# Delta-rule gates computed by channel and applied as the output leaves PSUM, with another fixed order of heads and dense blocks

## The chip, the core and the metric

The kernel runs on one core of a Trainium2 chip. A core has five engines with queues of their own: TensorE (matmuls and, beside them, weight loads), VectorE, ScalarE, GpSimd and SyncE, which issues the DMAs. Each engine works through its queue in program order. The metric is the device time of one execution in microseconds; the times given are medians of several runs, and the profile is of one further execution.

## What is computed

One decoder block for 512 tokens and a width of 1024: a Mamba-2 SSD mixer (8 groups) and a gated-delta-rule mixer (8 pairs of heads) side by side, merged by sigmoid gates, then a squared-ReLU MLP. The part that the change touches is the end of the delta-rule mixer, cut here to what matters:

```python
def gated_deltanet_branch(qkv, z, b, a, conv_w, dt_bias, A_log, norm_w):
    qkv = jax.nn.silu(causal_depthwise_conv(qkv, conv_w))
    ...
    o = gated_delta_rule_chunked(q, k, v, g, beta)      # (B, S, 16 heads, 128)
    o = rmsnorm(o, norm_w) * jax.nn.silu(z.reshape(Bsz, S, GDN_N_V_HEADS, GDN_HEAD_V).astype(f32))
    return o.reshape(Bsz, S, GDN_VAL_DIM).astype(z.dtype)
```

Here `z` is a slice of the input projection `h @ w_in`, and `norm_w` has one number for each of the 128 channels of a head. For each token and head the output is divided by its root mean square, multiplied by the channel's weight and by `silu(z)`.

## The kernel before

Weights and activations are float32. A dense product is made of three matmuls of rounded parts (`mm3`, L149 to L152): high times high, low times high, high times low. Each weight tile of 128x1024 is loaded by a DMA, its high part is made by ScalarE (L469, `whi`) and its low part by VectorE (L471, `wlo`). Weights use three buffers in rotation.

The kernel has two stages. The second (L1197 on: up-projections, output projection, MLP) is plain code. The first, in which the mixers run, is written as a set of Python generators, the "streams", which issue instructions and yield what they cost and what they wait for. A planner (class `Weave`) runs these streams against its own table of costs (`A`, `V`, `G`, `PE`, `DM`) while the kernel is built. At each step it takes the stream of the lowest rank that is ready in its own time. The order in which instructions are issued this way is fixed for every engine; on the chip nothing is reordered. Costs in the table thus move no work by themselves, but they decide which instruction stands ahead of which.

The streams, by rank: loads and normalisation at the front; `prologue` (decays); `heads(gdn_scan, ssd_scan)`, the scans one after the other; `heads(gdn_end, ssd_end)`, their ends; `heads(gdn_prep, ssd_prep)`, their preparation; `weights`, which loads and splits weights in the order in which they are used; `early_ch`, six dense blocks accumulated while inputs still arrive; last `dense`, the filler of TensorE.

There are 16 heads: 0 to 7 are pairs of delta-rule heads, 8 to 15 SSD groups. `ORDER` says in which order they go through scan, end and preparation. `SEQ` is the order of the dense blocks: `i3` is the input of the head at place 3 of `ORDER` (four blocks of 128 channels by 512 tokens, each followed by a convolution of four taps), `z3` its gate, and `g0` to `g12` are blocks of the merge gates, which only go to DRAM and can stand anywhere. Three more blocks of that kind (L1231 on) are done at the start of the second stage.

What ties dense blocks to heads: `dense_in` waits for the scan of the head four places ahead (L566), `dense_z` for the end of the head three places ahead (L597), since gates have three buffers. `gdn_end` and `ssd_end` wait for the gate of their own head.

A delta-rule head: `gdn_prep` transposes keys, queries and values and forms the matrices; `solve` inverts 32x32 blocks on GpSimd (L825, L827), between a DMA through DRAM (`btd`, then `Nb`, L816, one buffer) and another one back (`ubd`, then `U`, also one buffer, which waits for the scan before); `gdn_scan` (L858 to L947) extends the inverse to 128 rows and carries the state over four chunks; `gdn_out` adds up the outputs `o` (tokens on partitions). `gdn_end` then makes the norm `ro` (one number per token and head) and, in eight operations of VectorE (L999), multiplies `o` by `ro` and by the gate `zs`. TensorE transposes the product to channels (L1005), and `put_y` takes it out of PSUM on ScalarE with the channel's weight as its scale (L715) and sends it to DRAM (L718). An SSD head ends in the same way with operations of its own (L1156 to L1172, then `put_y`).

The gate block `dense_z` computes `zs` with tokens on partitions: for each of four groups of 128 tokens the activations are the stationary operand and 256 columns of the weight are moving, so a head takes 4 x 8 x 3 = 96 matmuls of 256 columns. `z_end` (L622) applies the SiLU. At the end of the last gate blocks the plan puts two sums of `w_ada` (L485, L487, on VectorE) between the weights of `z15` and the next dense weight.

Of the kernel before, what the change touches and what calls it, by code (L numbers as in the profile page):

```python
# [10 lines left out]
F32 = mybir.dt.float32  # L11
F32R = mybir.dt.float32r
AF = mybir.ActivationFunctionType
# [4 lines left out]
ADD, SUB, MUL, MAX, POW = ALU.add, ALU.subtract, ALU.mult, ALU.max, ALU.pow  # L18
# [3 lines left out]
P = 128  # L22
T = 512
NC = 4
D = 1024
KD = 8
EPS = 1e-6
NEG = -1e30
CC, CB, CN1, CN2, CSB, CAL, CSN, CGN, CCV = 0, 8, 40, 48, 56, 57, 58, 74, 75
NCOL = CCV + 64 * 5  # L30
ORDER = (0, 8, 1, 2, 9, 3, 10, 4, 11, 5, 12, 6, 7, 13, 14, 15)
SEQ = ("i0 g0 g1 g2 i1 z0 i2 z1 g3 g4 i3 z2 i4 z3 i5 z4 i6 z5 i7 z6 i8 z7 i9 z8 i10 z9 i11 z10 i12 z11 i13 z12 i14 z13 i15 z14 g5 g6 g7 z15 g8 g9 g10 g11 g12")


class Weave:
# [62 lines left out]
def A(n, k=1, f="A"):  # L98
    return f, k * (0.27 + n / 1330)


def V(n, k=1):
    return "V", k * (0.19 + n / 975)
# [6 lines left out]
def PE(t):  # L110
    return "P", t
# [5 lines left out]
def hybrid_block(ctx: ExitStack, tc: tile.TileContext, x, cols, drow, rows, w_ada, w_ch, w_z,  # L117
                 w_up, w_out, w_mu, w_md, out):
    nc = tc.nc
    sc, ve, gp, pe = nc.scalar, nc.vector, nc.gpsimd, nc.tensor  # L120
# [11 lines left out]
    col = const.tile([P, NCOL], F32, name="col")  # L132
# [16 lines left out]
    def mm3(ps, lhs, rhs, first, last):  # L149
        pe.matmul(ps, lhsT=lhs[0], rhs=rhs[0], start=first, stop=False)  # L150
        pe.matmul(ps, lhsT=lhs[1], rhs=rhs[0], start=False, stop=False)  # L151
        pe.matmul(ps, lhsT=lhs[0], rhs=rhs[1], start=False, stop=last)  # L152
# [49 lines left out]
    sp = mix.enter_context(tc.tile_pool(name="sp", bufs=2))  # L202
# [13 lines left out]
    hT = [(chan_tile(), chan_tile()) for _ in range(KD)]  # L216
    ssx = const.tile([P, NC], F32, name="ssx")
    rsx = const.tile([P, NC], F32, name="rsx")
    wv = Weave()
# [4 lines left out]
    def bank(tag):  # L224
        key = yield from wv.slot(tag, pb[tag])
        return key, (psd if tag == "ps" else pss).tile([P, T], F32, tag=tag, name=tag, bufs=pb[tag])
# [315 lines left out]
    pre, mid, gate = {}, {}, {}  # L542
# [52 lines left out]
    def dense_z(i):  # L595
        if at[i] > 2:
            yield [("end", before(i, 3))]  # L597
        zs = sp.tile([P, NC, 256], F32, tag="zs", name="zs", bufs=3)
        ws = []
        for h in range(2):  # L600
            yield [("z", i, h)]
            ws.append(wts.pop(("z", i, h)))
        for tp in range(2):
            bk, ps = yield from bank("ps")
            for th in range(2):
                ts = slice((2 * tp + th) * P, (2 * tp + th + 1) * P)
                for k in range(KD):
                    w = ws[k // 4]
                    ks = slice((k % 4) * 256, (k % 4 + 1) * 256)
                    mm3(ps[:, th * 256:(th + 1) * 256], (hT[k][0][:, ts], hT[k][1][:, ts]),  # L610
                        (w[0][:, ks], w[1][:, ks]), k == 0, k == KD - 1)
                    yield PE(0.36)
            wv.start(3, z_end(i, zs, tp, bk, ps))
        count()
        count()
# [3 lines left out]
            yield from {"in": dense_in, "z": dense_z, "g": dense_g}[kind](i)  # L619

    def z_end(i, zs, tp, bk, ps):
        sc.activation(zs[:, 2 * tp:2 * tp + 2, :], ps.rearrange("p (a b) -> p a b", a=2), AF.Silu)  # L622
        gate[i] = zs
        yield A(T, 1, "L")
        wv.mark(bk)
        wv.mark(("z", i, "end", tp))
# [82 lines left out]
        yield A(D, 1, "E")  # L709
        wv.mark(key)  # L710

    def put_y(slot, bk, ps, ncol):
        key = yield from wv.slot("y", 2)
        y = sp.tile([P, T], F32, tag="y", name="y", bufs=2)
        sc.activation(y, ps, AF.Copy, scale=ncol)  # L715
        yield A(T)
        wv.mark(bk)
        nc.sync.dma_start(out=ydr[slot], in_=y)  # L718
        yield DM
        wv.mark(key)  # L720
# [121 lines left out]
    def gdn_scan(hq):  # L842
# [11 lines left out]
        bk, ps = yield from bank("pb")  # L854
        Z1 = sp.tile([P, 8, 32], F32, tag="Z", name="Z1", bufs=1)
        for q in range(8):
            for b in (0, 64):
                pe.matmul(ps[b + 32:b + 64, q * 32:(q + 1) * 32], lhsT=btu[b:b + 32, q, b + 32:b + 64],  # L858
                          rhs=T6[b:b + 32, q, 0:32], start=True, stop=True, tile_position=(b, b + 32))
        yield PE(1.0)  # L860
        for b in (0, 64):
            sc.mul(Z1[b + 32:b + 64], ps[b + 32:b + 64, 0:256].rearrange("p (a b) -> p a b", a=8), -1.0)
        yield A(256, 2)
# [1 line left out]
        bk, ps = yield from bank("pb")  # L865
        for q in range(8):
            for b in (0, 64):
# [1 line left out]
                          rhs=U[b + 32:b + 64, q, b + 32:b + 64], start=True, stop=True, tile_position=(b + 32, b))  # L869
            pe.matmul(ps[32:64, 256 + q * 32:256 + (q + 1) * 32], lhsT=U[32:64, q, 32:64], rhs=Z1[32:64, q, :],  # L870
                      start=True, stop=True, tile_position=(32, 32))
        yield PE(1.55)
        ve.tensor_copy(out=T6[32:64, :, 0:32], in_=ps[32:64, 256:512].rearrange("p (a b) -> p a b", a=8))
        for b in (0, 64):
            ve.tensor_copy(out=U[b:b + 32, :, b + 32:b + 64], in_=ps[b:b + 32, 0:256].rearrange("p (a b) -> p a b", a=8))
# [2 lines left out]
        bk, ps = yield from bank("pb")  # L878
# [8 lines left out]
        bk, ps = yield from bank("pb")  # L887
# [9 lines left out]
        o = sp.tile([P, NC, 256], F32, tag="o", name="o")  # L897
        so = sp.tile([P, NC, 2], F32, tag="so", name="so", bufs=3)
        S = None
        for c in range(NC):  # L900
            if c:
                bk, psk = yield from bank("pb")
# [4 lines left out]
                for j in range(2):  # L907
                    js = slice(j * P, (j + 1) * P)
                    ve.scalar_tensor_tensor(out=r[:, js], in0=psk[:, js], scalar=neg[:, c, 2 * hq + j:2 * hq + j + 1],
                                            in1=vt[:, c, js], op0=MUL, op1=ADD)  # L910
                kqs = yield from wv.slot("qs", 2)
                qs = sp.tile([P, 256], F32, tag="qs", name="qs")
                for j in range(2):
                    js = slice(j * P, (j + 1) * P)
                    sc.activation(qs[:, js], psk[:, 256 + j * P:256 + (j + 1) * P], AF.Copy,
                                  scale=tok2[:, c, 32 + 2 * hq + j:33 + 2 * hq + j])
# [6 lines left out]
            for j in range(2):  # L923
                js = slice(j * P, (j + 1) * P)
# [9 lines left out]
            if c < NC - 1:  # L934
                yield V(256, 2)
                wv.mark(bku)
                bk, pst = yield from bank("pb")
# [3 lines left out]
                if c:  # L941
                    for j in range(2):
                        js = slice(j * P, (j + 1) * P)
                        hd = 32 + 2 * hq + j
                        ve.scalar_tensor_tensor(out=Sn[:, js], in0=S[:, js], scalar=elast[:, hd, c:c + 1],
                                                in1=pst[:, js], op0=MUL, op1=ADD)
# [31 lines left out]

    def gdn_end(hq):
        yield [("scan", hq)]  # L980
        for tp in range(2):
            yield [("z", hq, "end", tp)]
        for c in range(NC):
            yield [("o", hq, c, "end")]
        zs = gate.pop(hq)
        o, so, rq, ko = mid.pop(hq)
        rqb = rq[:, :, None].to_broadcast([P, NC, 2])
        ve.tensor_mul(out=so, in0=so, in1=rqb)
        ve.tensor_mul(out=so, in0=so, in1=rqb)
        ve.tensor_scalar(out=so, in0=so, scalar1=1.0 / P, scalar2=EPS, op0=MUL, op1=ADD)  # L990
        yield V(8, 3)
        ro = sp.tile([P, NC, 2], F32, tag="ro", name="ro")
        gp.tensor_tensor(out=ro, in0=so, in1=mhalf.rearrange("p (a b) -> p a b", a=NC), op=POW)
        yield ("G", 2.0)
        ve.tensor_mul(out=ro, in0=ro, in1=rqb)
        for c in range(NC):
            for j in range(2):
                js = slice(j * P, (j + 1) * P)
                ve.scalar_tensor_tensor(out=o[:, c, js], in0=o[:, c, js], scalar=ro[:, c, j:j + 1],  # L999
                                        in1=zs[:, c, js], op0=MUL, op1=MUL)  # L1000
            yield V(P, 2)
        for j in range(2):
            bk, ps = yield from bank("pb")
            for c in range(NC):
                pe.transpose(ps[:, c * P:(c + 1) * P], o[:, c, j * P:(j + 1) * P], ident)  # L1005
            yield PE(0.43)
            if j:
                wv.mark(ko)
            wv.start(3, put_y(2 * hq + j, bk, ps, col[:, CGN:CGN + 1]))
        wv.mark(("end", hq))  # L1010

    def ssd_prep(g):
        i = 8 + g
# [217 lines left out]
    for i in range(NG, 16):  # L1231
        ps = proj_ch(65 + i)
# [7 lines left out]
    for br in (1, 0):  # L1240
        if not br:
            ys = load_y(0)
        for m4 in range(2):
            pp = [lpsum() for _ in range(4)]
            for kq in range(4):
                for m2 in range(2):
                    w = dense_w(w_up[br, 2 * m4 + m2, kq])
                    for k in range(4):
                        kk = kq * 4 + k
                        for i in range(2):  # L1250
                            ws = slice(k * 256 + i * P, k * 256 + (i + 1) * P)
# [81 lines left out]
    for half in range(2):  # L1333
        tt = (2 * half, 2 * half + 1)
        for hf in range(2):
            for t in tt:
                pp[t, hf] = lpsum()
            for kp in range(4):
                w = dense_w(w_out[hf, kp])
# [21 lines left out]
    for q in range(4):  # L1361
        act = []
        for m in range(8):
            mm = q * 8 + m
            if mm < len(ups):
                ps = ups[mm][1]
# [158 lines left out]
```

## Time and profile before

| | |
|---|---|
| median of 3 runs | 1485.68 us (1484.53 to 1488.55) |
| the profiled execution | 1484.77 us |
| its span, first to last instruction | 1483.1 us |
| first stage up to the end of the early blocks | 0 to 69 us |
| rest of the first stage, to the last head's transposes | 69 to 878 us |
| second stage | 878 to 1483 us |
| mean granted TensorE clock | 0.996 of full speed |

Busy times are of one engine each and overlap. A group's row names the line, the engine, the operation, what is written and read and the shape, then the busy time, the mean duration of one, and the time that its engine stood idle before it with what ended that. A matmul's duration is longer than its distance to the next one, since matmuls are pipelined: the cost of one in a row of them is the distance between starts. A row of the waits gives who waited for whom, the total, how often and the longest.

### The profile page before, as it was taken

To read this page: it belongs to the slowest core of one execution; us is meant where nothing else is said; L and a number is where in the kernel's file an instruction comes from. 1 tells how busy PE (TensorE), PEld (TensorE's weight loads), DVE (VectorE), ACT (ScalarE), POOL (GpSimd) and SP (SyncE) were. 2 spreads that over 40 slices of the span, in tenths; PEclk is the share of its full clock that TensorE was granted. 3 is DMA by queue.
4 is the path that set the end of the run, shared out by engine and by line. 5 is a ranking of instruction groups with operands and counts; after the bars stand their busy time and mean duration, and the time that the engine had idled before them with its cause. 6 is when DMAs were issued, how large, how long until landed. Compare 5 with 4: busy or idle time off the path is not lost. (4 is left out here: it accounts for less than half of the span.)

```text
span 1483.1 us, 22692 instructions
## 1 busy us (share of the span) xinstructions
PE 1458.1 (98%) x8592; PEld 1241.0 (84%) x8592; DVE 862.5 (58%) x1522; ACT 732.6 (49%) x1379; POOL 370.2 (25%) x691
## 2 busy tenths in 40 slices
PE   9999999999999999999999899999999999999998
PEld 7788898879989889888888788888878888888886
DVE  3565577677767777676777634444477324343444
ACT  6575545673764747645665635333355333132232
POOL 3005444341814607336623410000011000000002
PEclk9999999999999999999999999999999999999999
DMA  9323434543434524344343449543372233223221
GB/s 360 127 97 118 150 103 125 128 137 97 151 119 138 158 81 151 121 116 138 116 137 119 158 170 331 175 156 127 110 239 88 97 100 100 89 96 99 93 95 69
DMA packets 87070, 199.47 MB, mean 134 GB/s; under 512 B 32504, under 2 KB 33024, under 8 KB 86960
## 3 DMA queue, kind: packets, MB, share of 16 engines
q1 hardware_dynamic: 86960, 198.01, 41.3%
q8 instruction: 68, 1.11, 0.3%
q14 instruction: 42, 0.34, 0.1%
HBM read 181.10 MB, written 16.88 MB: 133 GB/s over the span
## 5 line engine op out<-in xcount | busy, mean ns | idle before, releaser
L150 PE MATMUL ps<-hT,whi 128*128 128x512 f32 x688 | 285.7, 415 | 4.8 <-ACT whi L469 4.3
L151 PE MATMUL ps<-hT,wlo 128*128 128x512 f32 x688 | 269.8, 392 | 1.2 <-DVE wlo L471 1.2
L152 PE MATMUL ps<-hT,whi 128*128 128x512 f32 x688 | 269.9, 392 | 0.0
L146 DVE TENSOR_TENSOR wlo<-raw,whi 128x1024 fp32r<-128x1024 f32 x114 | 140.0, 1229 | 199.7 <-ACT whi L145 199.7
L145 ACT CAST whi<-raw 128x1024 fp32r<-128x1024 f32 x114 | 119.4, 1048 | 210.1 <-PE pl L151 61.9
L150 PE MATMUL ps<-whi,hT 128*128 128x256 f32 (+1 forms) x536 | 166.3, 310 | 2.2 <-ACT y L715 1.4
L471 DVE TENSOR_TENSOR wlo<-raw,whi 128x1024 fp32r<-128x1024 f32 x103 | 128.1, 1244 | 64.2 <-ACT whi L469 60.3
L150 PEld LDWEIGHTS ps<-hT,whi 128*128 128x128 f32 x688 | 129.9, 189 | 31.9 <-ACT whi L469 4.5
L152 PE MATMUL ps<-wlo,hT 128*128 128x256 f32 (+1 forms) x536 | 154.3, 288 | 0.6 <-DVE wlo L471 0.6
L151 PE MATMUL ps<-whi,hT 128*128 128x256 f32 (+1 forms) x536 | 153.8, 287 | 0.0
L152 PEld LDWEIGHTS ps<-hT,whi 128*128 128x128 f32 x688 | 129.7, 189 | 28.3
L151 PEld LDWEIGHTS ps<-hT,wlo 128*128 128x128 f32 x688 | 130.1, 189 | 25.8 <-DVE wlo L471 2.4
L469 ACT CAST whi<-raw 128x1024 fp32r<-128x1024 f32 x103 | 107.3, 1044 | 67.4 <-PE ps L152 47.1
L533 DVE SCALAR_TENSOR_TENSOR cv<-ps,col,cv 128x511 f32<-128x511 f32 (+1 forms) x180 | 133.0, 742 | 8.0 <-ACT cv L527 5.4
L150 PEld LDWEIGHTS ps<-whi,hT 128*128 128x128 f32 x536 | 102.1, 190 | 5.8 <-ACT y L715 1.6
L825 POOL TENSOR_TENSOR tm<-Ub,Nb 128x60 f32<-128x60 f32 (+24 forms) x248 | 93.7, 378 | 52.5 <-DMA Nb<-btd 37.6
L151 PEld LDWEIGHTS ps<-whi,hT 128*128 128x128 f32 x536 | 102.1, 190 | 2.2
L152 PEld LDWEIGHTS ps<-wlo,hT 128*128 128x128 f32 x536 | 101.8, 190 | 2.0 <-DVE wlo L471 0.8
L827 POOL TENSOR_TENSOR Ub<-Ub,tm 128x60 f32<-128x60 f32 (+24 forms) x248 | 95.0, 383 | 19.4
L1416 POOL TENSOR_TENSOR ya<-ya,gate 128x512 f32<-128x512 f32 x4 | 5.8, 1466 | 324.8 <-ACT junk L1414 324.8
L150 PE MATMUL pl<-hT,whi 128*128 128x512 f32 (+1 forms) x184 | 66.6, 363 | 1.0 <-DVE hT L195 1.0
L151 PE MATMUL pl<-hT,wlo 128*128 128x512 f32 (+1 forms) x184 | 66.1, 362 | 0.4 <-DVE wlo L146 0.4
(502 smaller groups left out, 3049.0 us busy)
## 6 DMA issues: line engine op xcount, KB each, us to landing
raw<-in_w_ch SPq DMA_DIRECT2D x81, 512.0 KB
raw<-in_w_ada SPq DMA_DIRECT2D x48, 512.0 KB
raw<-in_w_z SPq DMA_DIRECT2D x32, 512.0 KB
raw<-in_w_up SPq DMA_DIRECT2D x32, 512.0 KB
raw<-in_w_mu SPq DMA_DIRECT2D x32, 512.0 KB
raw<-in_w_md SPq DMA_DIRECT2D x32, 512.0 KB
dc<-acd SPq DMA_DIRECT2D x16, 512.0 KB
ydr<-y SPq DMA_DIRECT2D x32, 256.0 KB
```

The lines of the kernel that those rows point to most:

```text
L145: sc.copy(hi, raw)
L146: ve.tensor_sub(out=lo, in0=raw, in1=hi.bitcast(F32))
L150: pe.matmul(ps, lhsT=lhs[0], rhs=rhs[0], start=first, stop=False)
L151: pe.matmul(ps, lhsT=lhs[1], rhs=rhs[0], start=False, stop=False)
L152: pe.matmul(ps, lhsT=lhs[0], rhs=rhs[1], start=False, stop=last)
L469: sc.copy(hi, raw)
L471: ve.tensor_sub(out=lo, in0=raw, in1=hi.bitcast(F32))
L533: ve.scalar_tensor_tensor(out=t[:, s:], in0=ps[:, :T - s], scalar=col[:, o + k:o + k + 1], in1=t[:, s:], op0=MUL, op1=ADD)
L825: gp.tensor_tensor(out=t3, in0=Ub[:, 0:r, j:j + 1].to_broadcast([P, r, n]), in1=Nb[:, j:j + 1, j + 1:32].to_broadcast([P, r, n]), op=MUL)
L827: gp.tensor_tensor(out=Ub[:, 0:r, j + 1:32], in0=Ub[:, 0:r, j + 1:32], in1=t3, op=SUB)
L1416: gp.tensor_tensor(out=y, in0=y, in1=gates[1][:, hs], op=MUL)
```

## The change

Four things are changed.

- **Gates of delta-rule heads by channel.** For heads 0 to 7 `dense_z` makes the weight the stationary operand and moves 512 tokens, as the other dense blocks do. `zs` then has the channels on partitions, one 512-token row for each of the two heads of a pair. SSD heads keep their form.
- **The gate is applied on the way out of PSUM.** `gdn_end` multiplies `o` by the norm in two operations of 512 columns, ahead of its wait for the gate; `put_y` gets the gate as an argument and, for delta-rule heads, evacuates on VectorE: PSUM times the channel's weight times the gate. The mark that the head has ended is set there, once the second output has left PSUM, in place of the end of `gdn_end`.
- **Another fixed order.** `ORDER` puts delta-rule heads 0 to 4 first, then SSD heads 8 to 11, then 5, 6, 7, then 12 to 15. `SEQ` moves the gate blocks and spreads the g blocks: `z0` comes directly behind `g0`, and one g block, `g12`, follows `z15`, where five did.
- **Two costs in the planner's table** for the scan's first matmuls: 1.0 becomes 0.79, 1.55 becomes 0.65.

```diff
@@ -28,8 +28,9 @@
 NEG = -1e30
 CC, CB, CN1, CN2, CSB, CAL, CSN, CGN, CCV = 0, 8, 40, 48, 56, 57, 58, 74, 75
 NCOL = CCV + 64 * 5
-ORDER = (0, 8, 1, 2, 9, 3, 10, 4, 11, 5, 12, 6, 7, 13, 14, 15)
-SEQ = ("i0 g0 g1 g2 i1 z0 i2 z1 g3 g4 i3 z2 i4 z3 i5 z4 i6 z5 i7 z6 i8 z7 i9 z8 i10 z9 i11 z10 i12 z11 i13 z12 i14 z13 i15 z14 g5 g6 g7 z15 g8 g9 g10 g11 g12")
+ORDER = (0, 1, 2, 3, 4, 8, 9, 10, 11, 5, 6, 7, 12, 13, 14, 15)
+SEQ = ("i0 g0 z0 g1 g2 i1 i2 g3 z1 i3 g4 z2 g5 i4 i5 z3 g6 z4 i6 z5 i7 z6 i8 z7 i9 i10 z8 i11 g7 z9 g8 z10 "
+       "i12 z11 i13 g9 z12 i14 g10 z13 i15 z14 g11 z15 g12")
 
 
 class Weave:
@@ -595,13 +596,21 @@
     def dense_z(i):
         if at[i] > 2:
             yield [("end", before(i, 3))]
-        zs = sp.tile([P, NC, 256], F32, tag="zs", name="zs", bufs=3)
+        zs = sp.tile([P, 2, T] if i < 8 else [P, NC, 256], F32, tag="zs", name="zs", bufs=3)
         ws = []
         for h in range(2):
             yield [("z", i, h)]
             ws.append(wts.pop(("z", i, h)))
         for tp in range(2):
             bk, ps = yield from bank("ps")
+            if i < 8:
+                for k in range(KD):
+                    w = ws[k // 4]
+                    ks = slice((k % 4) * 256 + tp * P, (k % 4) * 256 + (tp + 1) * P)
+                    mm3(ps, (w[0][:, ks], w[1][:, ks]), hT[k], k == 0, k == KD - 1)
+                    yield PE(0.68)
+                wv.start(3, z_end(i, zs, tp, bk, ps))
+                continue
             for th in range(2):
                 ts = slice((2 * tp + th) * P, (2 * tp + th + 1) * P)
                 for k in range(KD):
@@ -619,7 +628,10 @@
             yield from {"in": dense_in, "z": dense_z, "g": dense_g}[kind](i)
 
     def z_end(i, zs, tp, bk, ps):
-        sc.activation(zs[:, 2 * tp:2 * tp + 2, :], ps.rearrange("p (a b) -> p a b", a=2), AF.Silu)
+        if i < 8:
+            sc.activation(zs[:, tp, :], ps, AF.Silu)
+        else:
+            sc.activation(zs[:, 2 * tp:2 * tp + 2, :], ps.rearrange("p (a b) -> p a b", a=2), AF.Silu)
         gate[i] = zs
         yield A(T, 1, "L")
         wv.mark(bk)
@@ -709,12 +721,18 @@
         yield A(D, 1, "E")
         wv.mark(key)
 
-    def put_y(slot, bk, ps, ncol):
+    def put_y(slot, bk, ps, ncol, z=None, end=None):
         key = yield from wv.slot("y", 2)
         y = sp.tile([P, T], F32, tag="y", name="y", bufs=2)
-        sc.activation(y, ps, AF.Copy, scale=ncol)
-        yield A(T)
+        if z is None:
+            sc.activation(y, ps, AF.Copy, scale=ncol)
+            yield A(T)
+        else:
+            ve.scalar_tensor_tensor(out=y, in0=ps, scalar=ncol, in1=z, op0=MUL, op1=MUL)
+            yield V(T)
         wv.mark(bk)
+        if end:
+            wv.mark(end)
         nc.sync.dma_start(out=ydr[slot], in_=y)
         yield DM
         wv.mark(key)
@@ -857,7 +875,7 @@
             for b in (0, 64):
                 pe.matmul(ps[b + 32:b + 64, q * 32:(q + 1) * 32], lhsT=btu[b:b + 32, q, b + 32:b + 64],
                           rhs=T6[b:b + 32, q, 0:32], start=True, stop=True, tile_position=(b, b + 32))
-        yield PE(1.0)
+        yield PE(0.79)
         for b in (0, 64):
             sc.mul(Z1[b + 32:b + 64], ps[b + 32:b + 64, 0:256].rearrange("p (a b) -> p a b", a=8), -1.0)
         yield A(256, 2)
@@ -869,7 +887,7 @@
                           rhs=U[b + 32:b + 64, q, b + 32:b + 64], start=True, stop=True, tile_position=(b + 32, b))
             pe.matmul(ps[32:64, 256 + q * 32:256 + (q + 1) * 32], lhsT=U[32:64, q, 32:64], rhs=Z1[32:64, q, :],
                       start=True, stop=True, tile_position=(32, 32))
-        yield PE(1.55)
+        yield PE(0.65)
         ve.tensor_copy(out=T6[32:64, :, 0:32], in_=ps[32:64, 256:512].rearrange("p (a b) -> p a b", a=8))
         for b in (0, 64):
             ve.tensor_copy(out=U[b:b + 32, :, b + 32:b + 64], in_=ps[b:b + 32, 0:256].rearrange("p (a b) -> p a b", a=8))
@@ -978,11 +996,8 @@
 
     def gdn_end(hq):
         yield [("scan", hq)]
-        for tp in range(2):
-            yield [("z", hq, "end", tp)]
         for c in range(NC):
             yield [("o", hq, c, "end")]
-        zs = gate.pop(hq)
         o, so, rq, ko = mid.pop(hq)
         rqb = rq[:, :, None].to_broadcast([P, NC, 2])
         ve.tensor_mul(out=so, in0=so, in1=rqb)
@@ -993,12 +1008,14 @@
         gp.tensor_tensor(out=ro, in0=so, in1=mhalf.rearrange("p (a b) -> p a b", a=NC), op=POW)
         yield ("G", 2.0)
         ve.tensor_mul(out=ro, in0=ro, in1=rqb)
-        for c in range(NC):
-            for j in range(2):
-                js = slice(j * P, (j + 1) * P)
-                ve.scalar_tensor_tensor(out=o[:, c, js], in0=o[:, c, js], scalar=ro[:, c, j:j + 1],
-                                        in1=zs[:, c, js], op0=MUL, op1=MUL)
-            yield V(P, 2)
+        for tp in range(2):
+            cs = slice(2 * tp, 2 * tp + 2)
+            o4 = o[:, cs, :].rearrange("p c (j b) -> p c j b", j=2)
+            ve.tensor_mul(out=o4, in0=o4, in1=ro[:, cs, :, None].to_broadcast([P, 2, 2, P]))
+            yield V(T)
+        for tp in range(2):
+            yield [("z", hq, "end", tp)]
+        zs = gate.pop(hq)
         for j in range(2):
             bk, ps = yield from bank("pb")
             for c in range(NC):
@@ -1006,8 +1023,7 @@
             yield PE(0.43)
             if j:
                 wv.mark(ko)
-            wv.start(3, put_y(2 * hq + j, bk, ps, col[:, CGN:CGN + 1]))
-        wv.mark(("end", hq))
+            wv.start(3, put_y(2 * hq + j, bk, ps, col[:, CGN:CGN + 1], zs[:, j, :], ("end", hq) if j else None))
 
     def ssd_prep(g):
         i = 8 + g
```

## The prediction

> **What bounds the kernel now.** I read the page first, then the busy time of each engine by stretch, then the waits of TensorE, then TensorE's groups by shape, then its timeline.
>
> ```profile
> PE 1458.1 (98%) x8592; PEld 1241.0 (84%) x8592; DVE 862.5 (58%) x1522; ACT 732.6 (49%) x1379; POOL 370.2 (25%) x691
> ...
> 69.00:878.00 809.00, 797.96 (x5453) 698.31 (x5453) 560.91 (x1119) 472.86 (x1016) 333.67 (x648) 1.00 0.41 126
> ```
>
> The second row (columns: length, then busy us and count of PE, PEld, DVE, ACT, POOL, then clock, DMA share, GB/s) is the stage in which everything changed here runs, from the end of the early blocks to the last head. TensorE is busy 798 of its 809 us; VectorE 561, ScalarE 473, GpSimd 334. So only two things can change the time: how much TensorE has to do, and how long it stands still. The second is small, and TensorE's waits list nearly all of it (columns: us in total, times, longest):
>
> ```profile
> PE ps L150 <- ACT whi L469: 4.3, 1, 4.3
> PE ps L150 <- DVE cv L533: 1.4, 2, 0.8
> PE ps L150 <- ACT y L715: 1.4, 1, 1.4
> PE ps L151 <- DVE wlo L471: 1.2, 3, 0.6
> ...
> PE pb L1005 <- DVE o L999: 1.1, 2, 0.7
> PE pb L858 <- DVE T L851: 0.8, 2, 0.6
> PE ps L152 <- DVE wlo L471: 0.6, 1, 0.6
> ```
>
> Together 10.8 us. The largest stands at the end of the stage, after the last gate block, and costs more than itself:
>
> ```profile
> 832.50:837.00 4.50, 0.25 (x3) 0.05 (x1) 4.27 (x7) 4.37 (x11) 4.03 (x4) 0.97 0.74 233
> 837.00:843.00 6.00, 5.51 (x12) 3.98 (x13) 3.76 (x4) 4.17 (x7) 1.02 (x1) 0.50 0.52 175
> ```
>
> TensorE idles, and in the 6.0 us after that the granted clock is 0.50: another 3.0 us of lost work. The end of the stage thus costs 4.3 + 3.0 = 7.3 us. The Trainium skill ("TensorE: Matmul & The Clock Gate", section on the HAM clock gate) says that the array falls to half its clock after an idle window of about 3.4 us; these rows agree (4.3 us idle, then 0.50).
>
> **The gate product by channel.** For the eight delta-rule heads, 96 matmuls of 256 columns become 48 of 512: 768 against 384. The spacing of each form, from runs that nothing interrupts (first and last row of 18 and of 24 records):
>
> ```profile
> 304.95 0.28 PE L150 MATMUL ps<-whi,hT 128*128 128x256 f32 x1
> ...
> 306.98 0.28 PE L152 MATMUL ps<-wlo,hT 128*128 128x256 f32 x1
> ```
>
> ```profile
> 878.44 0.39 PE L150 MATMUL ps<-hT,whi 128*128 128x512 f32 x1
> ...
> 883.65 0.39 PE L152 MATMUL ps<-hT,whi 128*128 128x512 f32 x1
> ```
>
> 2.03 us / 17 = 0.1194 us for 256 columns, 5.21 / 23 = 0.2265 for 512. Two narrow ones cost 0.2388, one wide one 0.0123 less: 384 x 0.0123 = **4.7 us saved**. The reason shows in two stretches, one of narrow and one of wide matmuls:
>
> ```profile
> 109.00:114.00 5.00, 5.00 (x45) 5.00 (x43) 3.33 (x9) 1.23 (x2) 1.45 (x2) 1.00 0.44 123
> ...
> 878.00:893.50 15.50, 15.50 (x70) 12.84 (x69) 6.62 (x8) 8.11 (x13) 0.00 (x0) 1.00 0.77 260
> ```
>
> The weight load is busy all 5.00 us with narrow matmuls and 12.84 of 15.50 with wide ones: narrow ones have nothing left under which a load can hide.
>
> The Trainium skill ("TensorE: Matmul & The Clock Gate", section "Back-to-back issue gap") gives a warm gap of the columns at 2.4 GHz plus 2.5 ns. By that the saving would be 384 x 2.5 ns, some 1.0 us as an estimate. The trace's spacing is above it in both forms and more so in the narrow one, so the measured 4.7 stands.
>
> What the plain spacing leaves out is the price of coming back to a dense block after another piece of work:
>
> ```profile
> L150 PE MATMUL ps<-hT,whi 128*128 128x512 f32 x688 | 285.7, 415 | 4.8 <-ACT whi L469 4.3 <-DVE cv L533 0.6
> ...
> L152 PE MATMUL ps<-hT,whi 128*128 128x512 f32 x688 | 269.9, 392 | 0.0
> L150 PE MATMUL ps<-whi,hT 128*128 128x256 f32 x512 | 156.8, 306 | 2.2 <-ACT y L715 1.4 <-DVE cv L533 0.8
> ...
> L151 PE MATMUL ps<-whi,hT 128*128 128x256 f32 x512 | 144.5, 282 | 0.0
> ```
>
> The first matmul of a triple is on the mean 23 ns longer than a later one at 512 columns, 24 ns at 256. If that stays per triple, 256 triples become 128 and 128 x 0.024 = 3.1 us more go: 7.8 saved. If the same pieces break into half as many triples, and each return is dearer by up to 0.1 us (my estimate: the 256 narrow triples carry 6.1 us of it, some 75 returns at 0.08, so up to 7.5 us), it ends 2.8 us dearer. I keep 4.7, the uninterrupted spacing, which lies between.
>
> **The gate multiplied on the way out.** For each head, eight 128x128 products on VectorE (L999) go, two 128x512 multiplications by the norm come, and the two evacuations of the output (`put_y`, L715) go from ScalarE to VectorE as one operation that also gates.
>
> ```profile
> L999 DVE SCALAR_TENSOR_TENSOR o<-o,ro,zs 128x128 f32<-128x128 f32 x64 | 29.4, 499 | 0.3
> ...
> L800 DVE TENSOR_TENSOR vt<-pa,srk 128x512 f32<-128x512 f32 x16 | 11.0, 685 | 4.9 <-PE pa L795 4.9
> ...
> L1377 DVE SCALAR_TENSOR_TENSOR sq<-ps,rl 128x512 f32<-128x512 f32 x12 | 8.3, 692 | 32.2 <-ACT rl L1375 32.2
> ...
> L715 ACT ACTIVATE y<-pb,col 128x512 f32<-128x512 f32 x32 | 20.2, 684 | 8.5 <-PE pb L1172 8.0 <-PE pb L1005 0.5
> ```
>
> VectorE: minus 29.4, plus 16 x 0.685 = 11.0 and 16 x 0.692 = 11.1, so 7.3 us less. ScalarE: 16 x 0.684 = 10.9 us less. Both lie under TensorE's 798 us and count for nothing by themselves. They do touch two waits: the transposes on `o` (1.1 us) and the bank behind `y` (1.4 us). The scaling now runs before the wait for the gate, and the transposes no longer read the gate at all. At best both waits go (2.5 us), at worst none does; I take **2.0**. The new operation waits on VectorE for the transposes; behind it in that queue stand the weight splits (L471) and the convolution taps (L533), on which TensorE waits 1.8 and 1.4 us today. That is its price if the cover goes, some 3 us. The output's DMA and its queue stay the same.
>
> **The order at the front.** z0 now follows g0 directly, ahead of g1 and g2, whose weights are loaded early. Its weights become the first of the streamed loads:
>
> ```profile
> 69.06 0.39 PE L150 MATMUL ps<-hT,ew 128*128 128x512 f32 x1
> ...
> 56.07 1.23 DVE L471 TENSOR_TENSOR wlo<-raw,whi 128x1024 fp32r<-128x1024 f32 x1 [0.34 <-ACT whi L469]
> 59.11 1.22 DVE L471 TENSOR_TENSOR wlo<-raw,whi 128x1024 fp32r<-128x1024 f32 x1 [1.21 <-issue]
> ```
>
> The early blocks end at 69.06; the first two streamed weights are split by 57.3 and 60.3. z0 waits for nothing: **0**.
>
> **The order in the middle.** Five delta-rule heads now come in a row, where they alternated. Their chain holds one buffer, `Nb`, from the DMA that fills it to the end of the solve on GpSimd:
>
> ```profile
> 115.34 0.68 SPq L816 DMA_DIRECT2D Nb<-btd  x1
> ...
> 127.12 0.24 POOL L825 TENSOR_TENSOR tm<-Ub,Nb 128x31 f32<-128x31 f32 x1 [3.64 <-DMA Nb<-btd]
> ...
> 165.35 0.21 POOL L827 TENSOR_TENSOR Ub<-Ub,tm 128x8 f32<-128x8 f32 x1
> ...
> 715.73 0.24 POOL L825 TENSOR_TENSOR tm<-Ub,Nb 128x31 f32<-128x31 f32 x1 [7.67 <-DMA Nb<-btd]
> ...
> 749.85 0.21 POOL L827 TENSOR_TENSOR Ub<-Ub,tm 128x8 f32<-128x8 f32 x1
> ```
>
> The load takes 11.8 us, the solve 38.4 (34.3 for the last head), so 46 to 50 us per head. Against that, TensorE's work per such head: four blocks of 24 wide matmuls, 21.7 us; a gate block, 10.9; other pieces: 798 less 72 blocks (391 us) and 16 gate blocks (183) is 224, 14 for each of 16 heads; and seven g blocks (5.4 each) spread over five heads, 7.6. That is 54 us. TensorE stays the slower by 4 to 8 us a head: **0**, with the ends 3.5 us better (the remaining waits of the list) and 15 worse (below).
>
> **The order at the end.** Before, five g blocks follow z15; now one does. What the last head's chain needs:
>
> ```profile
> 790.13 0.60 PE L1026 MATMUL pa<-ident,kq 128*128 128x128 f32 x4
> ...
> 816.42 0.60 PE L1098 MATMUL pb<-xw,bt__8707 128*128 128x256 f32 x2
> ...
> 832.47 0.28 PE L152 MATMUL ps<-wlo,hT 128*128 128x256 f32 x1
> ...
> 852.70 0.59 PE L1098 MATMUL pb<-xw,bt__8977 128*128 128x256 f32 x2
> ...
> 876.75 1.16 PE L1172 MATMUL pb<-ident,xk 128*128 128x128 f32 x8
> ```
>
> From preparation to scan 26 us (790.13 to 816.42, an SSD head that little else held), from scan to output transposes 24 (852.70 to 876.75); with some 6 for the convolution in front, 56 us from i15's last matmul. TensorE has in that time z14 and z15 (96 x 0.1194 each, 22.9 us), g11 and g12 (10.9) and some 1.25 heads' other work (17): 51. So about 5 us idle, where today 4.3 are lost, and the half clock after it as before; the last weight behind two sums of `w_ada`, which made TensorE wait for L469, keeps its place. I take **0.5 us worse**; bounds: 7.3 better, 33 worse (if the scan starts 20 us after z15 as it does now, 44 us of chain meet 5.4 of g12, less the 4.3 and a few us of its own work).
>
> Sum: -4.7 - 2.0 + 0 + 0 + 0.5 = -6.2. The profiled execution took 1484.77 us for a span of 1483.1; 1484.8 - 6.2 = 1478.6. The median of the runs shown, 1485.68, lies 0.9 above it, so **1479.5**.
>
> **Rivals.**
> 1. *The end is exposed, slower.* There is no filler after g12, and the order on each engine keeps the next stage's matmuls behind the last transposes. Price: if the last scan starts as z15 ends, 24 - 5.4 - 4.3 = 14 us more than today. It decides from about 14 us before z15's end; each us later costs one. -4.7 - 2.0 + 14 = +7: 1493. For it: today that scan starts 20 us after z15. Against: that lateness comes from two delta-rule heads just ahead of the last three, which the new order moves to the middle.
> 2. *The row of five is bound by its chain.* If a solve takes 60 us instead of 46 to 50, four heads lose some 5 us each, less slack: +15, 1494.
> 3. *No wait is left.* The 10.8 and the 3.0 us go with the 4.7 to 7.8: -18 to -22, 1464 to 1468. For it: all waits are short and hang on the order. Against: the last weight's place.
> 4. *The wide form saves nothing*, returns being dearer: +0 to -2: 1484.
>
> **Chances.** Forecast 0.47 (1473 to 1485), rival 1 0.18, rival 2 0.08, rival 3 0.15, rival 4 0.12. What a measurement can tell from no change is about 0.3%, 4.5 us: below 1481.2 or above 1490.1. Faster: two thirds of the forecast's (0.32), rival 3 (0.15), a little of rival 4 (0.03): 0.50. Slower: two thirds of rivals 1 and 2 (0.18) and a rest of 0.02: 0.20. Same: 0.30. Range 1466 to 1494: it takes in rivals 3 and 4 and most of 1 and 2.
>
> **What would show it.** Matmuls of `ps<-whi,hT` at 256 columns fall from 512 to 256 per line, those at 512 rise by 128, and uninterrupted spacing stays 0.2265: step one right. Waits on `o` and on `y` gone: step two. TensorE's wait on a weight after z15, the clock of 0.50 after it, and the distance from z15's last matmul to the last L1172 judge the end. A wait of L858 for the U DMA in the first 400 us would mean rival 2. I am wrong if TensorE's idle time in this stage changes by more than 5 us.

## The result and the profile after

| | before | after |
|---|---|---|
| median, runs of the same session | 1485.11 us (4 runs) | 1501.83 us (4 runs, 1497.83 to 1505.26) |
| ratio of the two | | 1.0107, 95% interval 1.0075 to 1.0139 |
| span of the profiled execution | 1483.1 us | 1498.5 us |
| mean granted TensorE clock | 0.996 | 0.991 |

The change makes the kernel slower by 1.1%, some 16 us. The forecast was 6.2 us faster, and the time lies above the range. Two views of the profile after, the busy times on its page and the stage in question by stretch (this stretch ends some 8 us into the second stage):

```profile
PE 1461.0 (97%) x8208; PEld 1223.7 (82%) x8208; DVE 858.1 (57%) x1490; ACT 717.2 (48%) x1356; POOL 358.5 (24%) x691
...
71.30:900.00 828.70, 807.92 (x5104) 687.26 (x5103) 558.67 (x1089) 460.37 (x998) 322.06 (x648) 0.99 0.41 126
```

TensorE has 384 matmuls fewer, as it should, and yet 3 us more of busy time. The waits of TensorE in the profile after say where it stands still (those of the first stage, in us in total, times, longest):

```profile
PE pb L907 <- ACT Z L902: 8.8, 2, 6.0
PE pb L886 <- ACT Z L880: 3.0, 2, 2.8
PE ps L152 <- DVE wlo L472: 2.8, 2, 2.4
PE ps L151 <- ACT whi L470: 2.7, 1, 2.7
PE pa L347 <- DMA raw<-in_w_ada: 2.0, 1, 2.0
...
PE pb L1022 <- DVE o L1014: 1.6, 1, 1.6
```

The two rows at the top are new: together 11.8 us in which the scan of a delta-rule head waits for `Z`, a copy of a block of the inverse out of PSUM by ScalarE. Neither stood in the list of before. The wait for the last weight is there as before (2.7 and 2.4 us), and the one on `y` is gone.

To see what each part weighs I took the starts of all matmuls between the first streamed dense block and the last transposes and split the distances: 0.2265 us for a dense matmul of 512 columns, 0.1194 for one of 256, and what goes beyond that.

| us | before | after | with the even load (e4) |
|---|---|---|---|
| stage | 808.6 | 820.3 | 802.3 |
| dense matmuls at those spacings | 574.8 | 570.1 | 570.1 |
| waits (over 0.45 us beyond the spacing) | 12.5 | 22.5 | 10.1 |
| return to a dense block (235, 244 and 244 times) | 28.3 | 30.6 | 29.5 |
| slower spacing inside blocks (half clock above all) | 5.9 | 8.4 | 6.5 |
| other matmuls, and ends of blocks | 187.1 | 188.7 | 186.1 |

The saving of 4.7 us is there to the tenth. The waits take 10.0 us more than before and the last three rows together 6.4. The third column has the same plan as the second: there the waits are 12.4 us less and the last three rows 5.6. Of the 15.4 us between the two spans, 11.7 are this stage; 2.2 lie ahead of it, where TensorE waits for the first `w_ada` load (2.0 us against 0.6). That start moved between 69.1 and 71.3 us in runs that have the same code up to there, so it is scatter; so are, I think, the 1.5 us of the second stage.

### One of the waits, followed back

TensorE after, around the first one:

```profile
179.13 0.39 PE L153 MATMUL ps<-hT,whi 128*128 128x512 f32 x1
182.35 0.24 PE L886 MATMUL pb<-U,Z 32*32 32x32 f32 x2 [2.83 <-ACT Z L880]
...
184.41 0.63 PE L153 MATMUL ps<-hT,whi 128*128 128x512 f32 x1
184.84 0.63 PE L151 MATMUL ps<-hT,whi 128*128 128x512 f32 x1
```

It idles 2.8 us; soon after it resumes, matmuls of 512 columns stand 0.43 us apart, half the speed. ScalarE and the DMA queue of SyncE in the same time:

```profile
180.26 1.04 ACT L470 CAST whi<-raw 128x1024 fp32r<-128x1024 f32 x1 [5.05 <-DMA raw<-in_w_ch]
181.92 0.78 ACT L880 ACTIVATE Z<-pb 32x256 f32<-32x256 f32 x2
...
164.54 1.80 SPq L856 DMA_DIRECT2D U<-ubd  x4
...
166.38 0.55 SPq L834 DMA_DIRECT2D Nb<-btd  x1
...
167.03 0.43 SPq L230 DMA_DIRECT2D raw<-in_w_ch  x1
```

ScalarE has stood for 5.05 us in front of a weight cast, and the Z copies are behind it in its queue. Z's own matmuls (L876) had started at 175.88. The weight, 512 KB, was issued at 167.03 and is used at 180.26, 13 us later. Ahead of it in the same queue are the small pieces of `U` and the load of `Nb`. What the 16 DMA engines do in the meantime:

```profile
171.00:176.00 5.00, 5.00 (x31) 3.89 (x31) 4.01 (x7) 3.15 (x15) 0.00 (x0) 1.00 0.97 191
176.00:181.00 5.00, 3.52 (x44) 2.64 (x42) 0.00 (x0) 0.74 (x1) 1.66 (x4) 1.00 0.30 92
```

In the last five microseconds before the cast they are busy 30% on the mean, at 92 GB/s. From 178 to 180 us the trace has four packets in flight, where it had 15 from 172 to 174: as if four engines still had work and the others none. (The trace does not name the engines.) The load of `Nb` takes as long elsewhere and in both kernels (11.8 us for 512 KB in the forecast's rows; after, issued at 118.58 and first used at 130.50). The other two waits have the same form with a decay load in place of the weight: issued at 277.37 and 667.62, each within 3 us behind an `Nb` load, awaited by ScalarE (L717) until 289.26 and 682.67, Z behind. The longest of the three, the load, ScalarE and TensorE:

```profile
667.62 0.94 SPq L712 DMA_DIRECT2D dc<-acd  x2
...
682.67 0.69 ACT L717 ACTIVATE dc<-dc,tok 128x128 f32<-128x128 f32 x2 [8.23 <-DMA dc<-acd]
...
685.88 1.97 PE L907 MATMUL pb<-U,Z 64*64 64x64 f32 x16 [5.99 <-ACT Z L902]
```

Here the DMA engines are busy almost to the end (share 1.00 from 676 to 680 us), so a few full engines alone do not describe it.

So there are three theories. **A**: the `Nb` load sits on a few DMA engines for 12 us, loads issued behind it are late, ScalarE stands in front of the late load with a copy behind it that TensorE needs; the order of before has such loads too, but nothing of that kind behind them. **B**: the two new planner costs put the scan's matmuls too near their copies. **C**: the gate, through VectorE's fuller queue.

### The profile page after: what moved, and what is told of

Same layout as the page of the kernel before. It is cut to its first block, busy times and chain, and to the rows that moved or that the text cites. A ratio compares the mean times of both kernels' runs of the same rounds, so it can differ in the third digit from the quotient of the medians.

```text
span 1498.5 us, 21881 instructions
## 1 busy us (share of the span) xinstructions
PE 1461.0 (97%) x8208; PEld 1223.7 (82%) x8208; DVE 858.1 (57%) x1490; ACT 717.2 (48%) x1356; POOL 358.5 (24%) x691
## 4 chain that ended last, share of the span: by engine, by line
PE 81%; DVE 7%; DMA 6%; ACT 2%; issue 2%; POOL 2%; SPq 0%; POOLq 0%; DVEq 0%; ACTq 0%
PE ps L151 15%; PE ps L152 14%; PE ps L153 14%; PE pl L153 7%; PE pl L151 7%; PE pl L152 7%; PE pb L1132 2%; DVE cv L534 2%; PE pb L922 1%; DVE wlo L472 1%; DMA dc<-acd 1%; PE pb L943 1%; DMA raw<-in_w_ch 1%; PE pb L979 1%; DMA rb<-in_rows 1%
## 5 line engine op out<-in xcount | busy, mean ns | idle before, releaser
L151 PE MATMUL ps<-hT,whi 128*128 128x512 f32 x816 | 345.7, 424 | 3.3 <-ACT whi L470 2.7
L152 PE MATMUL ps<-hT,wlo 128*128 128x512 f32 x816 | 321.0, 393 | 2.8 <-DVE wlo L472 2.8
L153 PE MATMUL ps<-hT,whi 128*128 128x512 f32 x816 | 321.5, 394 | 0.0
L151 PEld LDWEIGHTS ps<-hT,whi 128*128 128x128 f32 x816 | 154.8, 190 | 34.2 <-issue 3.6
L153 PEld LDWEIGHTS ps<-hT,whi 128*128 128x128 f32 x816 | 154.4, 189 | 34.4
L152 PEld LDWEIGHTS ps<-hT,wlo 128*128 128x128 f32 x816 | 155.1, 190 | 30.6 <-DVE wlo L472 3.8
L470 ACT CAST whi<-raw 128x1024 fp32r<-128x1024 f32 x103 | 107.6, 1045 | 71.3 <-PE ps L153 50.2
L843 POOL TENSOR_TENSOR tm<-Ub,Nb 128x60 f32<-128x60 f32 (+24 forms) x248 | 87.2, 352 | 71.8 <-DMA Nb<-btd 53.5
L845 POOL TENSOR_TENSOR Ub<-Ub,tm 128x60 f32<-128x60 f32 (+24 forms) x248 | 85.9, 347 | 19.4
L151 PE MATMUL ps<-whi,hT 128*128 128x256 f32 (+1 forms) x280 | 86.8, 310 | 0.0
L153 PE MATMUL ps<-wlo,hT 128*128 128x256 f32 (+1 forms) x280 | 81.9, 292 | 0.0
L152 PE MATMUL ps<-whi,hT 128*128 128x256 f32 (+1 forms) x280 | 81.6, 292 | 0.0
L151 PE MATMUL pl<-hT,whi 128*128 128x512 f32 (+1 forms) x184 | 66.6, 363 | 1.0 <-DVE hT L196 1.0
L153 PE MATMUL pl<-hT,whi 128*128 128x512 f32 (+1 forms) x184 | 66.1, 364 | 0.4 <-DVE hT L197 0.4
L151 PE MATMUL pl<-whi,act 128*128 128x512 f32 (+1 forms) x164 | 64.1, 391 | 0.0
L152 PE MATMUL pl<-whi,act 128*128 128x512 f32 (+1 forms) x164 | 64.0, 390 | 0.0
```

Source lines behind the costliest of these rows:

```text
L470: sc.copy(hi, raw)
L843: gp.tensor_tensor(out=t3, in0=Ub[:, 0:r, j:j + 1].to_broadcast([P, r, n]), in1=Nb[:, j:j + 1, j + 1:32].to_broadcast([P, r, n]), op=MUL)
L845: gp.tensor_tensor(out=Ub[:, 0:r, j + 1:32], in0=Ub[:, 0:r, j + 1:32], in1=t3, op=SUB)
```

## The experiments

### e1 to e3: the parts one by one

e1 is the changed kernel with the old `ORDER`, `SEQ` and costs, e2 the kernel before with the new `ORDER` and `SEQ`, e3 the changed kernel with

```diff
-        yield PE(0.79)
+        yield PE(1.0)
...
-        yield PE(0.65)
+        yield PE(1.55)
```

> The changed kernel with the order and the two planner costs of before: only the gates by channel and the gate on the way out. Theory A (the order is to blame: delta-rule heads in a row bring the U and Nb loads and a weight or decay load behind each other, the late load holds ScalarE, and TensorE waits for a copy behind it): faster than before by 4 to 8 us, 1477 to 1481. Theory B (the two planner costs are to blame: they put the scan's first matmuls too near their copies): also 1477 to 1481. Theory C (the gate itself is to blame, through VectorE's queue): 1495 or more.

Measured: 1490.67 us, ratio 1.0054 (1.0030 to 1.0079). Neither as A and B expected nor as slow as C. Its list of waits has one of 3.3 us on a SiLU, which e6 below has too.

> The kernel before with the new order of heads and dense blocks alone. Theory A: slower by 10 to 20 us, 1495 to 1505, with TensorE's waits on Z copies that stand behind a late load on ScalarE. Theories B and C: within 5 us of before, 1480 to 1490.

Measured: 1494.66 us, ratio 1.0071 (1.0048 to 1.0093). About the time that A expected, but the wait is not on Z copies; TensorE's and VectorE's longest waits in e2:

```profile
PE pb L882 <- DVE T L874: 7.0, 1, 7.0
...
DVE adacc L488 <- DMA raw<-in_w_ada: 10.3, 1, 10.3
```

Here it is VectorE that stands 10.3 us in front of a late load, with a copy for the scan behind it. That load was issued at 606.38, 0.6 us behind an `Nb` load, and was used at 620.13.

> The changed kernel with the two planner costs of before (1.0 and 1.55). Theory B: the waits of TensorE on Z copies (12 us) go, 1478 to 1488. Theories A and C: they stay or move, 1495 to 1505.

Measured: 1498.12 us, ratio 1.0091 (1.0068 to 1.0114); the wait on `Z L880` is 11.2 us. B falls.

Each part alone is a plan of its own: the planner deals all instructions anew, so parts need not add up, and a single part says little on the cause. (Here 0.5% and 0.7% alone and 1.1% together would agree with a sum; with the even load, in e4 to e7 below, they do not.) The next ones therefore keep the plan and change one transfer or one engine.

### e4 and e5: the Nb load spread evenly

```diff
-        nc.sync.dma_start(out=Nb.rearrange("p j i -> p (j i)"),
-                          in_=btd.rearrange("b u j i -> (b u) (j i)")[None].to_broadcast([4, 32, 1024]))
+        for h in range(4):
+            nc.sync.dma_start(out=Nb[h * 32:(h + 1) * 32].rearrange("p j i -> p (j i)"),
+                              in_=btd.rearrange("b u j i -> (b u) (j i)"))
```

e4 does this in the changed kernel, e5 in the one before. The same bytes move; the planner charges the same cost.

> The changed kernel with the Nb load issued as four DMAs of 32 partitions in place of one with a broadcast; the plan and the order of all other instructions stay. In the traces that load moves about 20 packets of 4 KB per us, some four DMA engines' worth, and takes about 12 us. Theory A: spread over more engines it lands in about 4 us, the loads behind it are not late, the three long waits of TensorE at 179, 288 and 679 us go with the half clock after them: 12 to 16 us faster than the changed kernel, 1484 to 1490. Theories B and C: no change, 1498 to 1505.

Measured: **1479.92 us**, ratio 0.9975 (0.9965 to 0.9985): 1.3% faster than the changed kernel's 1.0107. Both rows on Z copies are gone from TensorE's waits. What GpSimd waited for that load, after and in e4, and the cast and copy of above in e4:

```profile
POOL tm L843 <- DMA Nb<-btd: 53.5, 8, 11.4
```

```profile
POOL tm L844 <- DMA Nb<-btd: 9.7, 3, 6.1
```

```profile
173.14 1.05 ACT L470 CAST whi<-raw 128x1024 fp32r<-128x1024 f32 x1
174.09 0.68 ACT L530 ACTIVATE cv<-ps,col 128x512 f32<-128x512 f32 x1
174.80 0.78 ACT L881 ACTIVATE Z<-pb 32x256 f32<-32x256 f32 x2
```

The load behind `Nb` was issued at 165.82 in e4 and cast at 173.14: ScalarE waits for nothing there. Theory A holds for the three waits. B and C expected no change here: the new costs and the gate stay in e4, and the loss is gone.

> The kernel before with the Nb load issued as four DMAs of 32 partitions, its plan kept. Theory A as sharpened by e4 (a load behind Nb is late in both kernels, but only in the new order does ScalarE hold something for TensorE behind it): the kernel before lists no wait of TensorE on a Z copy, so it gains 0 to 4 us, 1480 to 1485. Rival (the even load is worth as much in any order, and e4 undid nothing of the change): it gains 15 us or more, under 1470.

Measured: 1483.32 us, ratio 0.9990 (0.9981 to 0.9999). The kernel before hardly gains, 0.1%: TensorE hardly waited for anything behind its late loads. The same edit is worth 1.3% in the changed kernel, so its loss is this meeting of late loads and copies; e7 below shows the same for the order alone.

### e6 and e7: e1 and e2 with the even load

> e1 (the gates alone, old order and costs) with the even Nb load. Theory A: what made e1 slower was the same late load; with it gone the gates give what the spacing of their matmuls says, some 4 to 7 us less than e5: 1474 to 1480. Theory C (VectorE's queue): stays at 1488 or more.

Measured: 1487.13 us, ratio 1.0023 (1.0011 to 1.0035). A miss: 3.5 us of e1's loss go, but no gain is left. In the same account as above its dense matmuls take the 4.7 us less, and its waits 14.1 us against 8.8 in e5. The longest in the list of e6:

```profile
PE ps L150 <- ACT whi L469: 4.5, 1, 4.5
PE ps L150 <- ACT zs L633: 3.1, 1, 3.1
```

The second is new: in that plan a dense block waits for the SiLU that empties its bank. ScalarE there:

```profile
585.27 0.59 ACT L1091 COPY xk<-pa 128x512 f32<-128x512 f32 x1 [2.82 <-DVE xd L1089]
...
588.11 0.60 ACT L633 ACTIVATE zs<-ps 128x512 f32<-128x512 f32 x1
```

The SiLU stands behind a copy that waits 2.8 us for VectorE, and no DMA is involved. The granted clock is then 0.50 from 588.8 to 594.6 us. So 3.1 us of waiting and 2.9 us of work lost to the half clock stand against the 4.7 us saved. That is read from the trace; no run took the wait away.

> e2 (the order alone) with the even Nb load. Theory A: the 10 us by which e2 was slower go, 1480 to 1487. Rival (the order itself costs, through the chain of the delta-rule heads): stays at 1490 or more.

Measured: 1484.08 us, ratio 0.9996 (0.9987 to 1.0006). The 0.7% of e2 are gone: the new order by itself, with the late loads taken out, costs nothing and gives nothing.

### e9: the Z copies moved to VectorE

The changed kernel, with the old `Nb` load:

```diff
-            sc.mul(Z1[b + 32:b + 64], ps[b + 32:b + 64, 0:256].rearrange("p (a b) -> p a b", a=8), -1.0)
+            ve.tensor_scalar_mul(Z1[b + 32:b + 64], ps[b + 32:b + 64, 0:256].rearrange("p (a b) -> p a b", a=8), -1.0)
...
-        sc.mul(Z2[64:128], ps[64:128, :].rearrange("p (a b) -> p a b", a=8), -1.0)
+        ve.tensor_scalar_mul(Z2[64:128], ps[64:128, :].rearrange("p (a b) -> p a b", a=8), -1.0)
```

> The changed kernel, Nb load as it is, with the three Z copies of each scan on VectorE in place of ScalarE; the plan and its order stay. Theory A says that TensorE waits because ScalarE is held by a late load with the Z copy behind it. At 288 and 679 us only ScalarE is held (by decay loads), so those two waits (9 us) and the half clock after them go; at 180 us VectorE is held too (by the weight split behind the late cast), so that one stays: 6 to 12 us faster than the changed kernel, 1490 to 1496. Rival (TensorE would be late anyway, for the U or Nb data itself): the waits stay, 1498 to 1505.

Measured: 1491.42 us, ratio 1.0047 (1.0030 to 1.0064). GpSimd waits for the `Nb` load as long as ever (51.8 us), yet about half of the loss goes, because the copy no longer stands behind the late loads on ScalarE. TensorE's waits in e9:

```profile
PE pb L922 <- DVE S L966: 3.6, 1, 3.6
...
PE pb L899 <- DVE T L891: 2.1, 1, 2.1
...
PE pb L886 <- DVE Z L880: 0.2, 1, 0.2
```

The wait on Z falls from 11.8 to 0.2 us; two shorter ones on VectorE come, at the first and the third of the three places. For the part that went, this run shows that TensorE waited because of ScalarE's queue, and not for `U` or `Nb` themselves.

### e8, e10, e11 and e12: the end of the stage

With the even load the largest waits left are those at the end, for the last weight. Its low part is made by VectorE. VectorE after, at that place:

```profile
878.05 3.90 DVE L488 SCALAR_TENSOR_TENSOR adacc<-raw,cact,adacc 128x256 f32<-128x256 f32 x6
881.87 1.22 DVE L472 TENSOR_TENSOR wlo<-raw,whi 128x1024 fp32r<-128x1024 f32 x1
```

Six operations of the `w_ada` sums stand in front of it. All four kernels are e4 with one change in the plan: e8 puts the second pair of sums at the gate of the ninth head in `ORDER` (`z8`, which is head 11); e10 ends `SEQ` with `z14 z15 g11 g12`; e11 with `i14 z13 i15 z14 g10 z15 g11 g12`; e12 puts the last two pairs of sums behind all weights:

```diff
-            for _ in range(2 if at[i] > 14 else at[i] > 0):
+            for _ in range(0 < at[i] < 15):
                 plan += [("a", (adas[0], hf), w_ada[2 * (8 + adas[0]) + hf]) for hf in range(2)]
                 adas.pop(0)
-    assert not adas, adas
+    for k in adas:
+        plan += [("a", (k, hf), w_ada[2 * (8 + k) + hf]) for hf in range(2)]
```

> e4 with one change in the plan: the second pair of w_ada sums stands with the gate of head 8 and not with the last gate block. The end of the stage loses 6 us to TensorE's waits on the last weight (L470, L472) and about 3 us to the half clock after them. If the two sums in front of that weight are the cause: both go, 1470 to 1474. If the place is not the cause: 1478 to 1483.

Measured: 1486.60 us, ratio 1.0009 (0.9999 to 1.0019). A miss. The waits on the last weight fell from 5.1 to 1.1 us, but the sums now hold something else; TensorE in e8, at the new place of the sums:

```profile
561.04 2.26 PE L1189 MATMUL pb<-ident,xk 128*128 128x128 f32 x8 [4.50 <-DVE xk L1183]
```

The granted clock is 0.50 from 560 to 566 us.

> e4 with g11 moved behind z15: two filler blocks after the last gate in place of one. e8 showed that with the weight wait gone the last transposes are late by some 5 us. If filler is what the end lacks: TensorE's idle time at the end falls, 1474 to 1479. If only the weight wait counts: 1478 to 1482.

> e4 with the input of the last head one block earlier and g10, g11 later (i14 z13 i15 z14 g10 z15 g11 g12). The last head's chain starts 5 us earlier and meets one block more: if the end is bound by that chain or lacks filler, 1473 to 1478; if only the weight wait counts, 1478 to 1482.

Measured: 1480.85 us (0.9985, 0.9974 to 0.9996) and 1480.43 us (0.9978, 0.9968 to 0.9988), both as e4. The weight wait stays in both (4.3 us on `wlo` in e10, 3.8 on `whi` in e11), so neither more filler nor an earlier last input takes it away.

> e4 with the last two pairs of w_ada sums behind the last dense weight in the plan in place of ahead of it; all earlier work keeps its plan. If those sums hold the last weight's split on VectorE: TensorE's two waits at the end (2.7 and 2.4 us) and the half clock after them go, less what the last transposes are then late (up to 5 us): 1473 to 1478. If the sums are not the cause: 1478 to 1482.

Measured: **1471.66 us**, ratio 0.9913 (0.9899 to 0.9927), better than expected and faster than both kernels. TensorE's longest waits of that stage in e12:

```profile
PE pb L1024 <- DVE o L1016: 1.6, 1, 1.6
PE pb L1190 <- DVE xk L1184: 1.3, 3, 0.7
```

The waits on the last weight are gone, all waits of the stage come to 4.2 us in the account, and the end is not exposed: the last transposes wait 0.2 us. No run puts the sums last in the kernel before, so this gain is not one of the change.

## Why the prediction was wrong

**The gate by channel: right.** Dense matmuls at the two spacings take 4.7 us less. The returns to a dense block, which the forecast left at zero between its bounds, cost 2.3 us more after and 1.2 more in e4: inside the bounds. But with the old order the gates gain nothing, even with the even load (e6). TensorE's first dense line in the profile after, beside the one before, has 816 matmuls of 512 columns against 688:

```profile
L151 PE MATMUL ps<-hT,whi 128*128 128x512 f32 x816 | 345.7, 424 | 3.3 <-ACT whi L470 2.7 <-DVE cv L534 0.6
...
L151 PE MATMUL ps<-whi,hT 128*128 128x256 f32 x256 | 77.3, 302 | 0.0
```

**The gate on the way out: half right.** The wait on `y` is gone, the one on `o` stays (1.6 us against 1.1): 0.9 of the 2.0 us. ScalarE is 15 us less busy. VectorE is 4 us less busy where 7.3 were forecast; its two new groups:

```profile
L1014 DVE TENSOR_TENSOR o<-o,ro 128x512 f32<-128x512 f32 x16 | 12.8, 797 | 0.3
L731 DVE SCALAR_TENSOR_TENSOR y<-pb,col,zs 128x512 f32<-128x512 f32 x16 | 11.3, 744 | 1.2 <-PE pb L1022 1.2
```

**The front: right.** z0 waits for no weight.

**The middle: the step that failed.** "TensorE stays the slower by 4 to 8 us a head: 0, with the ends 3.5 us better and 15 worse." The comparison of the chain with TensorE's work was sound as far as it went: rival 2 did not come, no scan waits for its solve. But the step put the waits of the middle at nothing, because it took the `Nb` load as a link of its own chain only. The row that gave 11.8 us for 512 KB was in the forecast; what it does to every load issued behind it was not asked, nor which engine stands in front of those loads, nor what TensorE needs from that engine next. That is three steps from the edited lines, and it cost 11.8 us of waits and the half clock after each (after, four places run at half speed; before, one).

The Trainium skill has the load's behaviour ("DMA: Bandwidth & Descriptors", "Rules for kernel authors"): the number of DMA engines that a transfer uses is set by its slowest dimension, and a leading broadcast of c copies confines it to at most c engines; `Nb` has a leading 4. The traces agree: 12 us for 512 KB, engines 30% busy behind it, and with four transfers of 32 partitions the lateness gone. A reader of that page would have had the first half of the mechanism, the confinement. That loads behind it come late, and what they then hold up, was to be read from the traces.

**The end: right in size, not by its reason.** Forecast 0.5 us worse: the waits there are 4.7 us before and 5.1 after, followed by 6.8 us at half clock in both. But the forecast expected about 5 us of idle time because the last head's chain (56 us) outlasts TensorE's work (51). The last transposes wait for nothing after, and the 5.1 us are the last weight alone, so the agreement is luck. Rival 1 did not come, and e12 shows that the end could spare its wait altogether.

**The sum.** -6.2 us was forecast for a stage in which nothing new waits. With the late loads taken out (e4) the stage is 6.3 us shorter than before, 802.3 against 808.6. That this is nearly the forecast is chance, since the even load shortens the stage of the kernel before as well (e5, 804.2). Against e5, which has the even load too, it is 1.9 us in the stage and 3.4 us in the medians: 1.1 us of returns, 1.3 of waits and 0.9 inside blocks come back out of the 4.7, and other matmuls take some 0.5 less.

Why e6, the gates alone, gains nothing is not shown: its trace names the wait on a SiLU and the half clock after it, and no run took that away.

## What to carry to other kernels

When work is put in another order, follow the transfers as well as the engines: which loads are issued behind the slow one now, which engine stops in front of them, and what else is in that engine's queue. A transfer whose duration is out of proportion to its bytes (12 us for 512 KB) can be a risk to another order, even if no wait in today's profile points at it. And where a planner deals all instructions anew, undoing parts of a change does not isolate them; change one transfer or one engine with the plan held fixed.

## What the runs showed of the hardware that was not expected

One DMA with a leading broadcast of 4 takes 12 us for 512 KB and delays a load issued 0.65 us behind it to 13 us; issued as four DMAs, the load behind is used 7 us after its issue, with nobody waiting.

The half clock does not come at once, and it does not go by the length of an idle time alone. After the idle time of 2.8 us that ended at 182.35 the granted clock was still 1.00 from 182.5 to 183.0; the clock records of the trace put the fall at 183.29. In every one of the fourteen traces the falls lie whole multiples of 3.41 us apart, and half speed lasts 3.41, 6.83 or 10.24 us, but for what the end of the execution cuts short. In the profile after, the 3.41 us ahead of two falls, the 3.41 us of the first half clock, and a stretch after which none came:

```profile
179.88:183.29 3.41, 0.79 (x48) 0.68 (x48) 1.89 (x2) 2.95 (x6) 3.02 (x6) 1.00 0.14 58
289.11:292.52 3.41, 1.11 (x17) 1.04 (x17) 0.00 (x0) 3.15 (x10) 2.67 (x10) 1.00 0.12 49
...
183.29:186.70 3.41, 3.41 (x23) 2.31 (x14) 2.75 (x5) 2.98 (x4) 2.63 (x10) 0.50 0.43 159
...
678.22:681.63 3.41, 1.67 (x8) 1.05 (x6) 0.65 (x1) 0.00 (x0) 0.82 (x4) 1.00 1.01 310
```

TensorE was busy for 0.79 and 1.11 of the 3.41 us before a fall, and for 1.67 where none came. Cut into such steps of 3.41 us between 60 and 1470 us, over all traces, each step at full clock in which it was busy under 46% was followed by half speed, none over 64% was, and between the two both happened. The Trainium skill ("TensorE: Matmul & The Clock Gate", section on the HAM clock gate) names an idle window of about 3.4 us; the length of 3.41 us agrees, but here the window did not have to be idle throughout.
